# Query and key projection with features on partitions, block-matrix mean squares, and weight low parts on GpSimd

## The chip, the cores and the metric

The kernel runs on one core of a Trainium2 chip. The metric is the device time of one launch in microseconds (us). The engines of the core are TensorE (PE in the profile; PEld is its weight load), VectorE (DVE), ScalarE (ACT), GpSimd (POOL) and SyncE (SP), which here only issues DMAs. Each engine takes its instructions in order; a "q" behind an engine's name means its queue. SBUF is the on-chip memory with 128 partitions, PSUM the memory into which TensorE accumulates.

## What is computed

One layer of a hybrid decoder on 1024 tokens with 1024 features, all in fp32. Cut to what matters here:

```python
h = rms_norm(x, attn_norm_w)
proj = h @ w_in                              # 7168 columns
q, k, v, u, g = jnp.split(proj, splits, axis=-1)
q = rms_norm(q.reshape(B, S, N_HEADS, 2, HEAD_DIM), q_norm_w)   # HEAD_DIM = 64
k = rms_norm(k.reshape(B, S, N_HEADS, 2, HEAD_DIM), k_norm_w)
# two softmaxes per head, over q1.k1 and q2.k2, each with a causal T5 bias; 8 heads
p = probs(qb1, k1f) - lamf * probs(qb2, k2f)
a = rms_norm(p @ v, subln_w) * (1.0 - lam_init)
# branch B: u_a * sigmoid(u_b), depthwise causal convolution of width 31, layer norm, silu, projection
# x + (g_a * y_a + g_b * y_b) @ w_out, then x + SwiGLU(rms_norm(x))
```

So each head has 128 columns of q and 128 of k, and each 64 of them are normalized by their own root mean square.

## The kernel before

**Products in three parts.** Each fp32 factor is split in a high part (fp32r, a cast on ScalarE, `split_hi`, L120) and a low part (source minus high part; `split_lo` on VectorE, L125, or GpSimd, L131, by the switch `low_by_pool` in `low`). A product is hi*hi + hi*lo + lo*hi, three matmuls for each slice of 128 along the contraction (`mm3`, L168 to L170). Two forms exist: `gemm_T` keeps 128 weight columns stationary and streams 512 tokens (the result has features on partitions); `gemm_N` keeps 128 tokens stationary and streams 256 weight columns (the result has tokens on partitions).

**Weights** come through the stream `ws`: a raw tile of 128x1024 by DMA on SP, the cast, the low part, in tiles `whi` and `wlo` of three buffers each; `ws.ahead` says how many are prepared in advance. `ld_cols` loads 128 columns whole, `ld_wide` 256 columns in two halves of the contraction.

**Stages.** First the norm of x, its transposes (`hT_hi`, `hT_lo`), v of the first columns; then v, and the u columns (`u_pair`, by a scheme of seven products per 2x2 blocks, L980), while the depthwise convolution runs on VectorE as background work `bg`: 31 taps (`conv_taps`, L594) for each of eight channel tiles. Taps of the first four tiles accumulate in PSUM (`CONV_PSUM = 4`), those of the others in SBUF. Through this stage `low_by_pool` is true. Then q and k of head 0 and the last v columns (`last`), then the attention.

**Attention** is a loop of 64 steps (8 heads x 8 tiles of 128 queries). A step does the scores of one tile (`scores`: two matmuls for each 512 keys, the bias and minimum on VectorE L1291, the exponential on ScalarE L1296, the difference of the two softmaxes on VectorE L1304 and L1306), turns the weights of the tile before (`turn`: transposes L1328, split L120 and L125), now and then sums v by them (`weigh`) and normalizes a head (`subln`, L1362), and takes a group of "fill" work from `later`: q and k of the next head (`q_item`) and the gate columns (`g_item`), 6 or 8 groups for each head. `turn` clears parts of `ph` and `pl` on GpSimd (L1318, L1319). The remaining 127 pieces of background work, taps of the last four tiles, are shared among the steps by a table of slack: `slack_of` estimates TensorE's and VectorE's time of each step. `low_by_pool` is false from here on.

**q and k of a head** (`q_item`): for each half of 512 tokens, four tiles of 128 tokens by `gemm_N` with 128 q and 128 k columns side by side; a copy to `qkraw` (L797), 16 sums of squares on ScalarE for each two tiles (L800), the root on VectorE and ScalarE (`rstd_of`, `rsq`), the scaling on VectorE (L807). `turn_qk` then transposes four 128x128 tiles on TensorE into PSUM (L815), and from there makes the high and low parts (L822, L824, L835), which DMAs on SP copy between the partition halves (8 for q, 2 for k). These are queued in `late` with the step from which their buffers are free.

A planner of the framework simulates the program and sets the order of instructions on each engine; `after(...)` in the code holds an instruction behind a given one. What the planner sets may differ between two programs in places that the diff does not name.

Of the kernel before, what the change touches and what calls it, by code (L numbers as in the profile page):

```python
# [16 lines left out]
P = 128  # L17
S = 1024
D = 1024
H = 8  # L20
# [37 lines left out]
def kernel(  # L58
# [170 lines left out]
    def load_vectors():  # L229
        pool.memset(rows[:], 0.0)  # L230
        pool.dma_start(cwrow[:], conv_w[0])
# [16 lines left out]
    neglam = cst.tile([P, 1], F32, name="neglam")  # L248
    lprod = ap.tile([P, 2, HD], F32, name="lprod", bufs=1)
# [34 lines left out]

    def wtiles():
        return [wp.tile([P, 1024], F32R, tag=t_, name=nm(t_)) for t_ in ("whi", "wlo")]
# [31 lines left out]
    def ld_wide(w, cols):  # L318


        def half(g):
            def go():
# [11 lines left out]
                hi, lo = wsplit(raw)  # L334
# [80 lines left out]

    def loads_of(it):
        c = int(it[1:])
        if it[0] == "V":
            return ld_wide(win, [(V0 + 256 * c, 256)])
# [224 lines left out]
    def rsq(v, n, fast):  # L644

        r = sm.tile([P, 16], F32, tag="r", name=nm("r"))[:, :n]
        t = sm.tile([P, 16], F32, tag="t", name=nm("t"))[:, :n]
# [32 lines left out]
    def rstd_of(ss, n, scale, fast=False):  # L680
        v = sm.tile([P, 16], F32, tag="v", name=nm("v"))[:, :n]
        dve.tensor_scalar(v, ss, scale, EPS, op0=ALU.mult, op1=ALU.add)
        return rsq(v, n, fast)
# [101 lines left out]

    def q_item(h):
        halves = [ws.next(), ws.next()]
        t = {}
        T[h] = t
        for b in (1, 0):  # L790
            raw = qkp.tile([P, 4, 256], F32, tag="qkraw", name=nm("qkraw"), bufs=2)
            ss = sm.tile([P, 16], F32, tag="ss16", name=nm("ss16"))
            for i2 in range(2):
                o = pg()
                for e in range(2):
                    gemm_N(o[:, 256 * e : 256 * (e + 1)], halves, hT_hi, hT_lo, 4 * b + 2 * i2 + e)
                act.copy(raw[:, 2 * i2 : 2 * i2 + 2, :], o[:].rearrange("p (e c) -> p e c", c=256))  # L797
                jk = sm.tile([P, VD], F32, tag="jk", name=nm("jk"), bufs=1)[:, :HD]
                for g in range(8):
                    act.activation(  # L800
                        jk, o[:, g * HD : (g + 1) * HD], AF.Square, accum_out=ss[:, 8 * i2 + g : 8 * i2 + g + 1]
                    )
                if i2 == 0:
                    yield
            r = rstd_of(ss[:], 16, 1.0 / HD, fast=h > 0)
            r4 = raw[:].rearrange("p i (g d) -> p (i g) d", d=HD)
            dve.tensor_tensor(r4, r4, r.unsqueeze(2).to_broadcast([P, 16, HD]), op=ALU.mult)  # L807

            def turn_qk(z, key, b, raw):


                dma = nc.sync.dma_start
                pt = pm("pQ")
                for i in range(4):
                    pe.transpose(pt[:, i * P : (i + 1) * P], raw[:, i, z * P : (z + 1) * P], ident[:])  # L815
                w = pcol(key + "n")

                def part(j):
                    return qkp.tile([P, 512], F32R, tag=f"{key}s{j}", name=f"{key}s{j}_{h}_{b}", bufs=2 if key == "q" else 3)

                s1, s2 = part(1), part(2)
                act.activation(s1[:], pt[:], AF.Identity, scale=w)  # L822
                lo = part(3) if key == "q" else qkp.tile([P, 512], F32R, tag="klo", name=f"klo_{h}_{b}", bufs=1)
                dve.scalar_tensor_tensor(lo[:], pt[:], w, f32(s1[:]), op0=ALU.mult, op1=ALU.subtract)  # L824
                if key == "q":
                    dma(f32(s2[HD:, :]), f32(s1[HD:, :]))
                    lo2 = part(4)
                    for one, two in ((s1, s2), (lo, lo2)):
                        if one is lo:
                            dma(f32(two[HD:, :]), f32(one[HD:, :]))  # L830
                        dma(f32(two[:HD, :]), f32(one[HD:, :]))
                        dma(f32(one[HD:, :]), f32(one[:HD, :]))
                    t["q", b] = (s1, lo), (s2, lo2)
                else:
                    act.activation(s2[HD:, :], pt[HD:, :], AF.Identity, scale=w[HD:, :])  # L835
                    dma(f32(s2[:HD, :]), f32(lo[HD:, :]))
                    dma(f32(s1[HD:, :]), f32(lo[:HD, :]))
                    t["k", b] = s1, s2

            for z, key in ((1, "k"), (0, "q")):
                free = NT * (h - 1) + (0 if key == "k" and b else NT if key == "q" and not b else NT // 2)
                late.append((free if h else 0, lambda a_=(z, key, b, raw): turn_qk(*a_)))
            yield
# [400 lines left out]
    while late:  # L1246
        late.pop(0)[1]()
# [887 lines left out]
```

## Time and profile before

| | us |
|---|---|
| median of 3 runs | 1726.78 |
| lowest, highest | 1726.03, 1735.44 |
| profiled execution, first to last instruction (span) | 1725.7 |
| TensorE busy | 1714.6 |
| VectorE busy | 1275.4 |
| ScalarE busy | 862.5 |
| GpSimd busy | 219.1 |

The span is of one profiled execution; its own time is not listed apart from it, and the median of the runs is 1.1 us above it. Busy time of TensorE counts matmuls from start to modelled end, and these overlap, so that it says little on how dense they stand; the distance from one start to the next does. In a row of a group, the first number behind the bar is the busy time of all instructions of the group in us, the second the mean of one in ns, the third the idle time of the engine ahead of them, with what ended it. In the chain, a row has its start, its length, and the group with its count. In the timeline, a row has its start and length in us, the engine, line, operation, and tiles, out<-in. The windows show the busy time of each engine in a stretch.

### The profile page before, as it was taken

How to read it: one execution, taken by the hardware profiler on the slowest of the kernel's cores; microseconds unless marked ns; L12 is line 12 of the kernel's file. 1: busy time of each engine (PE TensorE's matmuls, PEld its weight loads, DVE VectorE, ACT ScalarE, POOL GpSimd, SP SyncE). 2: the span in 40 equal slices, each digit the busy share in tenths (PEclk: the TensorE clock that was granted, in tenths of full speed). 3: DMA queues.
4: the chain of work that ended last, by engine and by line, in shares of the span. 5: the costliest groups of instructions: out<-in, count | busy, mean ns of one | idle time of the engine just before them, and what ended most of it. 6: DMA issues, size and time to landing. Idle time of an engine off the chain costs nothing.

```text
span 1725.7 us, 25863 instructions
## 1 busy us (share of the span) xinstructions
PE 1714.6 (99%) x9243; PEld 1477.9 (86%) x9243; DVE 1275.4 (74%) x2128; ACT 862.5 (50%) x1958; POOL 219.1 (13%) x207
## 2 busy tenths in 40 slices
PE   9999999999999999999999999999999999999999
PEld 7997889998998998988788888888888888888887
DVE  7675889898988888878687769966676666575544
ACT  5333335767777776756556325633333333333332
POOL 3997851000000000000000000000000000000000
PEclk9999999999999999999999999999999999999999
DMA  6344445336345344343973683245455445598663
GB/s 208 116 126 132 131 151 154 104 109 171 104 127 147 115 125 138 101 136 130 333 238 118 200 296 119 74 135 164 147 170 170 154 141 164 175 355 285 217 215 130
DMA packets 261604, 281.64 MB, mean 163 GB/s; under 512 B 16546, under 2 KB 181986, under 8 KB 261475
## 3 DMA queue, kind: packets, MB, share of 16 engines
q1 hardware_dynamic: 254160, 267.71, 48.3%
q0 software_dynamic: 5680, 9.39, 2.6%
q10 hardware_dynamic: 1634, 2.89, 0.5%
q8 instruction: 73, 1.20, 0.3%
q14 instruction: 57, 0.46, 0.1%
HBM read 181.84 MB, written 85.50 MB: 155 GB/s over the span
## 4 chain that ended last, share of the span: by engine, by line
PE 92%; DMA 3%; DVE 2%; ACT 1%; issue 1%; POOL 0%; SPq 0%; DVEq 0%; POOLq 0%; ACTq 0%
PE acc L980 29%; PE acc L488 12%; PE pg L168 12%; PE pg L169 12%; PE pg L170 12%; PE wo L1850 3%; PE sc L1290 2%; PE sc L1289 2%; PE pT L1328 2%; PE pg L1106 1%; DVE acc L594 1%; PE pW L168 1%; PE pW L169 1%; PE pW L170 1%; PE pQ L815 1%
## 5 line engine op out<-in xcount | busy, mean ns | idle before, releaser
L594 DVE SCALAR_TENSOR_TENSOR acc<-u,cw,acc 128x1023 f32<-128x1023 f32 (+14 forms) x240 | 303.4, 1264 | 23.2 <-ACT acc L588 20.7
L170 PE MATMUL pg<-whi,hT_lo 128*128 128x256 f32 x704 | 200.2, 285 | 0.0
L168 PE MATMUL pg<-whi,hT_hi 128*128 128x256 f32 x704 | 199.7, 285 | 0.4 <-DVE v L125 0.4
L169 PE MATMUL pg<-wlo,hT_hi 128*128 128x256 f32 x704 | 199.5, 284 | 0.0
L125 DVE TENSOR_TENSOR wlo<-draw,whi 128x1024 fp32r<-128x1024 f32 x75 | 91.7, 1223 | 83.4 <-ACT whi L120 78.9
L120 ACT CAST whi<-draw 128x1024 fp32r<-128x1024 f32 x75 | 79.1, 1055 | 129.5 <-PE acc L488 114.3
L169 PEld LDWEIGHTS pg<-wlo,hT_hi 128*128 128x128 f32 x704 | 134.4, 191 | 1.8
L170 PEld LDWEIGHTS pg<-whi,hT_lo 128*128 128x128 f32 x704 | 134.3, 191 | 1.8
L168 PEld LDWEIGHTS pg<-whi,hT_hi 128*128 128x128 f32 x704 | 134.0, 191 | 2.1 <-DVE v L125 0.6
L120 ACT CAST whi<-wraw 128x1024 fp32r<-128x1024 f32 x90 | 94.7, 1052 | 70.6 <-PE pg L169 32.6
L488 PE MATMUL acc<-wlo,whi 128*128 128x512 f32 x308 | 119.8, 389 | 0.0
L488 PE MATMUL acc<-whi,wlo 128*128 128x512 f32 x308 | 119.8, 389 | 0.0
L1296 ACT ACTIVATE E<-E,mn 128x640 f32<-128x640 f32 (+7 forms) x128 | 99.8, 781 | 30.8 <-DVE mn L1291 29.2
L168 PE MATMUL pg<-hT_hi,whi 128*128 128x512 f32 x288 | 114.4, 397 | 0.1
L169 PE MATMUL pg<-hT_lo,whi 128*128 128x512 f32 x288 | 113.7, 395 | 0.0
L170 PE MATMUL pg<-hT_hi,wlo 128*128 128x512 f32 x288 | 113.7, 395 | 0.0
L120 ACT CAST whi<-s 128x1024 fp32r<-128x1024 f32 x54 | 56.9, 1053 | 104.9 <-PE acc L980 101.8
L125 DVE TENSOR_TENSOR wlo<-wraw,whi 128x1024 fp32r<-128x1024 f32 x75 | 93.3, 1246 | 12.6 <-ACT whi L120 12.3
L1291 DVE CUSTOM_DVE_ANT_0 E<-sc,tb 128x512 f32<-128x512 f32 (+3 forms) x128 | 74.2, 585 | 33.2 <-PE pT L1328 16.1
L980 PE MATMUL acc<-h_hi,whi 128*128 128x512 f32 x240 | 93.4, 389 | 0.0
L980 PE MATMUL acc<-h_lo,whi 128*128 128x512 f32 x240 | 93.4, 389 | 0.0
L980 PE MATMUL acc<-h_hi,wlo 128*128 128x512 f32 x240 | 90.1, 389 | 0.0
(370 smaller groups left out, 4589.7 us busy)
## 6 DMA issues: line engine op xcount, KB each, us to landing
wraw<-in_w_gate_up_dram SPq DMA_DIRECT2D x44, 512.0 KB, 4.7
wraw<-in_w_in_dram SPq DMA_DIRECT2D x38, 512.0 KB, 4.0
qs<-qs SPq DMA_DIRECT2D x96, 128.0 KB, 2.3
wd<-in_w_down_dram SPq DMA_DIRECT2D x44, 256.0 KB, 3.1
tdT<-wd SPq DMA_DIRECT2D x88, 128.0 KB, 4.8
draw<-sdS SPq DMA_DIRECT2D x44, 256.0 KB, 3.7
draw<-tdT SPq DMA_DIRECT2D x44, 256.0 KB, 3.7
wraw<-in_w_in_dram SPq DMA_DIRECT2D x32, 256.0 KB, 3.3
```

The source lines that it names most:

```text
L120: act.copy(dst, src)
L125: last_lo[0] = dve.tensor_tensor(dst, src, f32(hi), op=ALU.subtract).ins
L168: pe.matmul(o, lh, rh, start=start, stop=False)
L169: pe.matmul(o, lh, rl, start=False, stop=False)
L170: last_mm[0] = pe.matmul(o, ll, rh, start=False, stop=stop).ins
L488: m = pe.matmul(o[s_][i][:], l_[:, ts], r_[:, 512:], start=start and j + y_ == 0, stop=j == n - 1 and y_ == 2, skip_group_check=not start,)
L594: dve.scalar_tensor_tensor(a_, us[c][:, : S - n], cw[:, c, t : t + 1], a_, op0=ALU.mult, op1=ALU.add)
L980: last_mm[0] = pe.matmul(o[:], a_[x_][:, k, :], b_[y_][:, k, :], start=start and k + x_ + y_ == 0, stop=k == 3 and x_ == 1, skip_group_che ...
L1289: pe.matmul(o[:, :w], qh[:, qs], k, start=True, stop=False)
L1291: dve.tensor_tensor_reduce(e[:, ks], o[:, :w], tb[:, S - nk + c0 : S - nk + c0 + w], 1.0, mn[:, j : j + 1] if c0 else 3.0e38, ALU.add, ALU ...
L1296: act.activation(e[:, :nk], e[:, :nk], AF.Exp, bias=mn[:, j : j + 1], scale=-1.0, accum_out=l[:, j : j + 1])
L1850: last_mm[0] = pe.matmul(o[s_][i][:], A[u_], B[v_], start=start and j + y_ == 0, stop=j == 3 and y_ == 2, skip_group_check=not start,).ins
```

## The change

- `q_item` computes q and k by `gemm_T`: for k, then q, two halves of 512 tokens each; the weights are two loads of 128 columns (`ld_cols`) in place of two halves of 256. Each result is copied to a tile `raw` of 128 features x 512 tokens. No transposes remain in `turn_qk`; it reads `raw` in SBUF where it read PSUM.
- Mean squares: `qk_step`, once a step, takes one `raw`: the square and its upper bound (`BIGSQ`) on GpSimd, the high part on ScalarE, the low part on GpSimd. A step later (`LAG = 1`) `norm_qk` multiplies both by `halfmean`, a matrix of two 64x64 blocks of -0.5/64, so that PSUM holds -0.5 times the mean square of each feature's half on every partition; ScalarE takes the logarithm and the exponential, GpSimd scales `raw`, and three operations on VectorE do one Newton step.
- Low parts of weights stay on GpSimd through the attention (`low_by_pool` is reset only behind it).
- Buffers: three places of weight tiles by number; two serve as weights in the attention, with one tile ahead, the third as room for the squares and roots. The low and high parts of one v weight lie in the `pl` tile.
- The table of ScalarE's logarithm and exponential is loaded ahead of head 0's q and k. `slack_of` has new constants for VectorE.

```diff
     def loads_of(it):
...
         if it[0] == "Q":
-            return ld_wide(win, [(Q0 + c * P, P), (K0 + c * P, P)])
+            return ld_cols(win, K0 + c * P) + ld_cols(win, Q0 + c * P)
...
     def q_item(h):
...
+        T[h] = {}
+        for key in "kq":
+            w = ws.next()
+            for b in (1, 0):
+                o = gemm_T(w, hT_hi, hT_lo, b)
+                raw = qkp.tile([P, 512], F32, tag="raw", name=f"raw{key}{h}_{b}", bufs=4)
+                act.copy(raw[:], o[:])
+                raws.append((h, key, b, raw))
+                yield
...
+    def qk_step(n):
+        while norms and norms[0][0] <= n - LAG:
+            norm_qk(*norms.pop(0)[1])
+        if raws and len(norms) < 2:
+            h, key, b, raw = raws.pop(0)
+            hi, lo, place = q_room(F32R)
+            sq = apl[0].tile([P, 512], F32, tag="at", name=nm("sq"), bufs=2)[:]
+            pool.tensor_tensor(sq, raw[:], raw[:], op=ALU.mult)
+            pool.tensor_scalar(sq, sq, BIGSQ, None, op0=ALU.min)
+            split_hi(hi, sq)
+            pool.tensor_tensor(lo, sq, f32(hi), op=ALU.subtract)
+            norms.append((n, (h, key, b, raw, hi, lo, place)))
+
+    def norm_qk(h, key, b, raw, hi, lo, place):
+        pt = pm("pN")
+        pe.matmul(pt[:], halfmean[:], hi, start=True, stop=False)
+        last_mm[0] = pe.matmul(pt[:], halfmean[:], lo, start=False, stop=True).ins
+        r, t, _ = q_room(F32, place)
+        act.activation(r, pt[:], AF.Ln, scale=-2.0, bias=eps[:])
+        act.activation(r, r, AF.Exp, scale=-0.5)
+        pool.tensor_tensor(raw[:], raw[:], r, op=ALU.mult)
+        dve.scalar_tensor_tensor(t, pt[:], -0.5 * EPS, r, op0=ALU.add, op1=ALU.mult)
+        dve.tensor_tensor(t, t, r, op=ALU.mult)
+        dve.scalar_tensor_tensor(raw[:], t, 1.5, raw[:], op0=ALU.add, op1=ALU.mult)
...
     def turn_qk(h, key, b, raw):
...
+        act.activation(s1[:], raw[:], AF.Identity, scale=w)
...
+        dve.scalar_tensor_tensor(lo[:], raw[:], w, f32(s1[:]), op0=ALU.mult, op1=ALU.subtract)
...
     def first_stage():
...
-        ws.ahead = 2
+        tc.keep_in_program_order(act.preload_act_table_set("natural_log_exp_and_others"))
+        with after(last_of(mybir.EngineType.Activation)):
+            make_neglam()
+        wplace[0] = cycle((0, 1))
+        ws.ahead = 1
...
-    low_by_pool[0] = False
     pcv_ctx.close()
...
     def slot(n, nq):
         with after(last_fill[0]):
+            qk_step(n)
...
     def slack_of(n):
...
-        t_dve = 0.4 + 4.2e-3 * nk + p + 0.3
+        t_dve = 0.7 + 4.2e-3 * nk
+        if n < NT * (H - 1):
+            t_dve += (0.7, 3.5, 2.6, 1.9, 2.5, 1.4, 0.0, 0.0)[n % NT]
...
+        if n == NT * (H - 1) + 1:
+            wplace[0], ws.ahead = cycle((2, 1 - wlast[0], wlast[0])), 2
...
     inatt[0] = False
+    low_by_pool[0] = False
```

More of the change, by code (lines that the diff above doesn't have):

```diff
@@ L333, in go @@
                     o += n
-                hi, lo = wsplit(raw)
+                hi, lo = wsplit(raw, tiles[g])
                 return (
@@ L784 @@
     late = []
+    BIGSQ = 3.3e38
+    raws, norms, LAG = [], [], 1
     def q_item(h):
[L787 to L845, printed above, removed]
@@ L1245 @@
         due -= int(due)
+    while norms or raws:
+        qstep[0] += 1
+        qk_step(qstep[0])
     while late:
         late.pop(0)[1]()
-    low_by_pool[0] = False
     pcv_ctx.close()
```

68 lines of the change are left out of this document (55 added, 13 removed).

## Prediction

> **What bounds the kernel now.** I read the page's totals and the chain first, then the chain in order of time, then the busy times of the attention stretch.
>
> ```profile
> span 1725.7 us, 25863 instructions
> PE 1714.6 (99%) x9243; PEld 1477.9 (86%) x9243; DVE 1275.4 (74%) x2128; ACT 862.5 (50%) x1958; POOL 219.1 (13%) x207
> ...
> PE 92%; DMA 3%; DVE 2%; ACT 1%; issue 1%; POOL 0%; SPq 0%; DVEq 0%; POOLq 0%; ACTq 0%
> ```
>
> ```profile
> 147.85 94.99 PE acc L980 x418
> ...
> 405.06 0.44 PE pQ L815 x4
> ```
>
> ```profile
> core 0: us, PE busy (x) PEld busy (x) DVE busy (x) ACT busy (x) POOL busy (x), PEclk, DMA share, GB/s
> 240.00:306.00 66.00, 65.64 (x516) 63.99 (x515) 56.87 (x63) 32.98 (x104) 15.09 (x10) 1.00 0.65 181
> 306.00:812.00 506.00, 503.77 (x3366) 460.90 (x3366) 437.17 (x972) 358.84 (x1186) 17.88 (x69) 1.00 0.43 122
> ```
>
> TensorE holds 92% of the chain, at a granted clock of 1.00. A matmul row lasts longer than its turn, because matmuls overlap; the turn is what counts. In the chain 418 matmuls of 512 columns take 94.99 us, so one turn is 0.227 us. The 506 us from 306 to 812 are the attention, in which q and k of heads 1 to 7 are made, one head during the one before it: 63 us for each of 8 heads. There VectorE is busy 437.2 us, 86%, so it has only 68.8 us of idle time, and GpSimd has almost nothing to do (17.9 us). Time goes down if TensorE has fewer turns, as long as VectorE's 437 us and what it waits for stay under TensorE's time. That is the question of this change.
>
> **TensorE's sum.**
>
> ```profile
> 65.74 0.28 PE L169 MATMUL pg<-wlo,hT_hi 128*128 128x256 f32 x1
> ...
> 72.46 0.28 PE L168 MATMUL pg<-whi,hT_hi 128*128 128x256 f32 x1
> ```
>
> Between these two rows of the timeline lie 56 turns of 256 columns: 6.72 us, 0.120 us each. So two narrow turns (0.240) cost little more than a wide one (0.227), although their rows have long durations.
> - q and k: out go 8 heads x 8 token tiles x 8 slices x 3 = 1536 turns at 0.120, 184.3 us. In come 8 x 2 x 2 x 24 = 768 turns at 0.227, 174.5 us. Gain 9.8.
> - Transposes: out go 128 at 0.11 (0.44 for 4 in the chain), 14.1 us.
> - Mean squares: in come 64 products of 512 columns with the block matrix at 0.227, 14.5 us.
>
> Net 9.4 us less, 8.2 of them in the attention and 1.2 for head 0 ahead of it. TensorE alone would take 498 us in the attention.
>
> **ScalarE** loses the sums of squares:
>
> ```profile
> L800 ACT ACTIVATE jk<-pg 128x64 f32<-128x64 f32 x220 | 49.8, 226 | 4.8
> L800 ACT ACTIVATION_READ_ACCUMULATOR jk<-pg 128x1 f32 x220 | 43.9, 199 | 0.0
> L1296 ACT ACTIVATE E<-E,mn 128x512 f32<-128x512 f32 x16 | 11.6, 723 | 3.8 <-DVE mn L1291 3.8
> ```
>
> 93.7 us go. For each of the 28 blocks (7 heads, q and k, two halves) come a split, a logarithm and an exponential of 512 columns, at most 28 x 3 x 0.72 = 61 us. It was busy 359 of 506 us; it falls to some 326 and bounds nothing. The table load that moves ahead costs nothing there, for the same reason.
>
> **VectorE's own work** in the attention:
>
> ```profile
> L594 DVE SCALAR_TENSOR_TENSOR acc<-u,cw,acc 128x1023 f32<-128x1023 f32 (+14 forms) x120 | 151.2, 1260 | 2.9 <-ACT acc L588 2.8
> ...
> L1306 DVE SCALAR_TENSOR_TENSOR E<-E,rl,E 128x640 f32<-128x640 f32 (+7 forms) x63 | 51.6, 819 | 0.6
> ...
> L125 DVE TENSOR_TENSOR wlo<-wraw,whi 128x1024 fp32r<-128x1024 f32 x29 | 35.4, 1219 | 2.8 <-ACT whi L120 2.7
> ...
> L807 DVE TENSOR_TENSOR qkraw<-qkraw,r 128x1024 f32<-128x1024 f32 x14 | 17.0, 1218 | 0.0
> ...
> L1304 DVE SCALAR_TENSOR_TENSOR rl<-rl,neglam,l 128x1 f32<-128x1 f32 x64 | 13.7, 214 | 0.5
> L824 DVE SCALAR_TENSOR_TENSOR qs<-pQ,pvec,qs 128x512 fp32r<-128x512 f32 x14 | 10.4, 746 | 4.6 <-ACT qs L822 4.6
> ...
> L1362 DVE TENSOR_TENSOR an<-an,r 128x1024 f32<-128x1024 f32 x7 | 8.5, 1216 | 0.0
> L656 DVE TENSOR_SCALAR t<-t 128x16 f32<-128x16 f32 (+1 forms) x21 | 3.6, 173 | 0.2
> ```
>
> ```profile
> L963 DVE TENSOR_TENSOR s<-wraw,wraw 128x512 f32<-128x512 f32 x20 | 13.7, 684 | 0.0
> ```
>
> Out: the weights' low parts (35.4), the scaling of the raw tiles (17.0), and for 14 row norms five small operations of about 0.17, as L656 (11.9): 64.3 us. In: for each of 28 blocks two SCALAR_TENSOR_TENSOR of 512 columns (0.746, as L824) and one TENSOR_TENSOR (0.684, as L963): 61 us. VectorE's own work goes from 437 to 434 us. By itself that changes nothing.
>
> **GpSimd's new work, and what it does to VectorE.** GpSimd's rows from ahead of the attention, and its memsets in it:
>
> ```profile
> L131 POOL TENSOR_TENSOR wlo<-wraw,whi 128x1024 fp32r<-128x1024 f32 x15 | 36.2, 2414 | 49.6 <-ACT whi L120 49.6
> ...
> L131 POOL TENSOR_TENSOR sl<-wraw,sh 128x512 fp32r<-128x512 f32 x7 | 9.2, 1307 | 1.6 <-ACT sh L120 1.6
> ```
>
> ```profile
> L1319 POOL MEMSET pl<- 128x128 f32 x30 | 6.2, 206 | 440.2 <-PE pW L169 348.7 <-PE pW L170 38.1 <-DVE rl L1304 20.5
> ```
>
> 29 low parts at 2.41 are 70 us. Each of 28 blocks has three two-input operations of 512 columns (square, low part of the square, raw times r) at 1.31 and one minimum. The trace has no such minimum: between 0.21 (a memset of 128 columns) and 1.31 I take 1.0, nearer to the row of the same width. 28 x 4.93 = 138. Together 208 us (186 to 217) in 506: GpSimd itself has room. But see both engines where they met before:
>
> ```profile
> 46.60 9.47 POOL L896 TENSOR_TENSOR F<-hT_hi,hT_lo 128x1024 f32<-128x1024 f32 x4
> 56.04 9.09 POOL L905 TENSOR_TENSOR F<-F,F 128x1024 f32<-128x1024 f32 x3
> ...
> 271.12 4.77 POOL L131 TENSOR_TENSOR wlo<-wraw,whi 128x1024 fp32r<-128x1024 f32 x2 [17.17 <-ACT whi L120]
> ```
>
> ```profile
> 48.42 0.69 DVE L125 TENSOR_TENSOR vl<-pg,vh 128x512 fp32r<-128x512 f32 x1 [2.02 <-ACT vh L120]
> 49.02 4.78 DVE L272 TENSOR_TENSOR lprod<-lamt 128x64 f32<-128x64 f32 x2
> ...
> 56.94 2.57 DVE L125 TENSOR_TENSOR wlo<-wraw,whi 128x1024 fp32r<-128x1024 f32 x1
> ...
> 273.47 1.26 DVE L594 SCALAR_TENSOR_TENSOR acc<-u,cw,acc 128x1009 f32<-128x1009 f32 x1
> 274.65 2.31 DVE L807 TENSOR_TENSOR qkraw<-qkraw,r 128x1024 f32<-128x1024 f32 x1
> ```
>
> Two products of only 64 columns took 4.78 us beside L896: each stood for one whole GpSimd operation. L807 took 2.31 beside L131 where its group in the attention has 1.22, and the low part at 56.94 took 2.57 against 1.22. Each of these has both inputs in SBUF. The split at 48.42 and the tap at 273.47 (its acc is one of the four PSUM accumulators) read one input from PSUM and lost nothing. So while GpSimd reads SBUF, a VectorE operation with two SBUF inputs stands still until GpSimd's operation is over. The attention's taps (L594, accumulators in SBUF there), L1306, L1304, L1362 and the new operations with two SBUF inputs (TENSOR_TENSOR, the last SCALAR_TENSOR_TENSOR, and L824, which now reads SBUF) come to 151.2 + 51.6 + 13.7 + 8.5 + 28 x (0.684 + 0.746 + 0.746) = 286 us, 57% of the stretch. No row shows a large SCALAR_TENSOR_TENSOR with two SBUF inputs beside a reading GpSimd: its wait lies between nothing and that of the TENSOR_TENSOR rows. I take theirs, as the nearest form.
>
> The Trainium skill, "SBUF — State Buffer", section "Who interferes with whom", says that any VectorE instruction with two SBUF inputs contends with a GpSimd instruction that reads SBUF, and that the second one waits for the whole of the first. By that rule the taps wait too, and the sum is the one below; without it, it is that of the first rival. The rows above agree for TENSOR_TENSOR; none here shows it for the taps.
>
> How much of GpSimd's 208 us VectorE loses lies between none (each falls under an operation that reads PSUM, or idle time) and all. L807 lost 1.09 of an operation of 2.4, 0.46; the low part at 56.94 lost 1.35, 0.56. I take 0.5: 104 us.
>
> **The sum.** VectorE needs 434 + 104 = 538 us in the attention, TensorE 498. VectorE becomes the bound: its idle 69 us are gone and the stretch grows from 506 to 538, by 32 us. The gain of 8.2 is hidden under this. Ahead of it (240 to 306), where head 0 is made and the taps still accumulate in PSUM, VectorE gets 4 x 2.18 = 8.7 us and loses two L807 (2.31 and 1.22) and ten small operations (1.7): 3.5 more, with 9 idle; TensorE gains 1.2. I take 0 (-1.2 to +3.5). The new slack table moves taps to the last head, which the sum over all eight already allows. Behind 812 nothing changes in amount. The profiled execution's span is 1725.7, and the median, 1726.8, lies 1.1 above it, which I take as what surrounds the span: 1725.7 + 32 + 1.1 = **1759 us**. If VectorE cannot be filled beyond 94%, as in its fullest stretch here,
>
> ```profile
> 350.00:400.00 50.00, 50.00 (x363) 47.15 (x362) 46.88 (x96) 36.62 (x132) 1.71 (x7) 1.00 0.42 117
> ```
>
> it is 572 for 538, +66, 1793. The forecast's own range is 1736 to 1790.
>
> **Costed at nothing.** The 8 and 2 DMAs of each turned q and k block stay on SP, in the same number. The two halves of a wide weight load become two loads of the same bytes. The products with the block matrix are the added wait: behind them in TensorE's queue stand all later matmuls. They come a step (63 / 8 = 7.9 us) after the squares, whose chain on GpSimd and ScalarE is 1.31 + 1.0 + 0.72 + 1.31 = 4.3 us; if it is later than a step, TensorE waits for the rest. One weight ahead in place of two: a tile serves two steps, 15.8 us.
>
> ```profile
> L120 ACT CAST whi<-wraw 128x1024 fp32r<-128x1024 f32 x29 | 30.5, 1052 | 16.4 <-PE pg L169 13.5 <-PE pg L170 2.8
> ```
>
> ```profile
> wraw<-in_w_in_dram SPq DMA_DIRECT2D x38, 512.0 KB, 4.0
> ```
>
> Cast 1.05, load 4.0 and low part 2.41 are 7.5 us, which TensorE's matmuls of those two steps cover; with no cover each tile costs up to 7.5.
>
> **Rivals.**
> 1. *Only TENSOR_TENSOR waits; SCALAR_TENSOR_TENSOR does not.* Then the port touches L1362 and the new TENSOR_TENSOR, 28 us, plus small ones: 35 operations with at most 2.4 each, 84 us at worst and some 30 likely, where 498 - 434 = 64 are free. TensorE stays the bound: 1726.8 - 9.4 = 1717.4. For: only TENSOR_TENSOR is shown waiting. Against: the other form also reads two tensors from SBUF. It decides for "not slower". Chance 0.25, of which 0.17 are over 0.5% faster.
> 2. *The waits fall mostly into idle time.* At a lost share under (498 - 434) / 208 = 0.31 TensorE remains the bound (1717.4); up to 0.39 the time stays within 0.5% (8.6 us). For: taps often alternate with score operations that read PSUM. Against: 0.46 and 0.56 above. Chance 0.17: 0.06 faster, 0.11 the same.
> 3. *Low parts stick in GpSimd's queue.* The memsets of ph and pl wait for TensorE's weighted sums (440 us idle before 30 of them, 14.7 each); the engine takes its instructions in order, so a low part, and a square, behind such a memset waits too, and TensorE waits for the weight. With 8 us to spare per tile a stuck one costs some 7; a quarter of 29 costs 50: about 1767. Against: the planner can place a low part ahead of the memset. Chance 0.08, slower.
>
> The forecast has 0.50. Faster by over 0.5%: 0.17 + 0.06 = 0.23. Within 0.5%, about what a measurement of this kernel can tell from no change: 0.08 + 0.11 = 0.19. Slower: 0.50 + 0.08 = 0.58. The range 1714 to 1788 takes in rival 1 with its small spread and nearly all of the forecast's own range.
>
> **What would show it.** In the changed profile: pg groups of q and k at 512 columns, no pQ transposes, 1536 fewer narrow turns (right or wrong at once). Taps with a mean well over 1.26 us, and L1306's over 0.82, where GpSimd's share is high: the forecast's mechanism. Taps at 1.26: rival 1. VectorE over 95% busy from 306 on and TensorE's idle waits named DVE: the bound has moved. Waits of TensorE for GpSimd's low parts: rival 3. The forecast is wrong if the taps keep their duration, or if their waits stay under 64 us in all.

## The result, and the profile after

The changed kernel takes 1812.5 us (median of 4 runs, 1808.9 to 1813.1) beside 1726.4 us for the kernel before: a ratio of 1.048, 95% interval 1.0449 to 1.0511. It is 86 us slower. The forecast of 1759 us had the direction; the time lies above its range (1714 to 1788).

The page of the kernel after: totals, and the shares of the chain that ended last.

```profile
span 1807.1 us, 23873 instructions
...
PE 1750.3 (97%) x8411; PEld 1449.3 (80%) x8411; DVE 1357.0 (75%) x2096; ACT 844.0 (47%) x1511; POOL 489.6 (27%) x369
...
PE 54%; DVE 11%; DMA 2%; issue 2%; ACT 2%; POOL 0%; SPq 0%; DVEq 0%; ACTq 0%; POOLq 0%
```

In after the chain could be followed back only to 489.7 us, so its shares add up to 71% where those of before add up to 99%: 54% beside 92% is no fall of that size. Of the part that is covered TensorE has 54 of 71 and VectorE 11 of 71, where VectorE had 2 of 99. The windows of the kernel after, columns as in the prediction (PE, PEld, DVE, ACT, POOL, clock, DMA):

```profile
240.00:306.00 66.00, 66.00 (x383) 58.16 (x382) 60.66 (x61) 27.07 (x39) 38.77 (x28) 1.00 0.53 151
306.00:884.00 578.00, 531.05 (x2693) 441.81 (x2691) 518.04 (x946) 347.08 (x809) 264.12 (x210) 0.95 0.40 112
```

The attention takes 578 us in place of 506. VectorE's busy time rose from 437 to 518 us, and 60 us of idle time remain of 68.8. TensorE's granted clock is 0.95 where it was 1.00. VectorE's groups in that stretch:

```profile
L614 DVE SCALAR_TENSOR_TENSOR acc<-u,cw,acc 128x994 f32<-128x994 f32 (+14 forms) x121 | 182.8, 1511 | 7.8 <-ACT acc L608 7.5
L1337 DVE CUSTOM_DVE_ANT_0 E<-sc,tb 128x512 f32<-128x512 f32 (+3 forms) x128 | 74.3, 582 | 22.0 <-DMA tb<-t_d 8.9 <-PE sc L1336 8.0 <-PE pT L1374 3.9
L1352 DVE SCALAR_TENSOR_TENSOR E<-E,rl,E 128x640 f32<-128x640 f32 (+3 forms) x64 | 62.7, 979 | 0.9
...
L1350 DVE SCALAR_TENSOR_TENSOR rl<-rl,neglam,l 128x1 f32<-128x1 f32 x64 | 27.5, 430 | 0.8
L852 DVE TENSOR_TENSOR qroom<-qroom 128x512 f32<-128x512 f32 x28 | 27.5, 981 | 0.2
L851 DVE SCALAR_TENSOR_TENSOR qroom<-pN,qroom 128x512 f32<-128x512 f32 x28 | 19.1, 683 | 0.7 <-ACT qroom L849 0.7
...
L869 DVE SCALAR_TENSOR_TENSOR klo<-rawk,pvec,ks 128x512 fp32r<-128x512 f32 x14 | 14.9, 1061 | 2.2 <-ACT ks L867 2.2
L853 DVE SCALAR_TENSOR_TENSOR rawq<-qroom,rawq 128x512 f32<-128x512 f32 x14 | 13.2, 943 | 2.3 <-POOL rawq L850 1.2
L869 DVE SCALAR_TENSOR_TENSOR qs<-rawq,pvec,qs 128x512 fp32r<-128x512 f32 x14 | 13.1, 935 | 3.2 <-ACT qs L867 3.2
L853 DVE SCALAR_TENSOR_TENSOR rawk<-qroom,rawk 128x512 f32<-128x512 f32 x14 | 11.7, 833 | 0.5
```

The taps went from 1260 to 1511 ns, L1352 (L1306 before) from 819 to 979, L1350 from 214 to 430. L851, of the same width as L853 but with one input in PSUM, stays at 683. L1337, which reads the scores from PSUM, stays too (582 ns; L1291 before, 585). What lengthens reads two tensors from SBUF, and only where GpSimd reads at the same time: in the trace half of the taps lie beside such an operation of GpSimd and take 1765 ns on the mean, the other half 1262; L851 has 683 and 680. A small exception is L676, a TENSOR_SCALAR with one tensor from SBUF: the one of its seven that lies beside such a read takes 1.05 us, the others 0.17. Two places of the timeline, VectorE's rows first:

```profile
598.58 1.49 DVE L614 SCALAR_TENSOR_TENSOR acc<-u,cw,acc 128x995 f32<-128x995 f32 x1
...
600.40 3.37 DVE L614 SCALAR_TENSOR_TENSOR acc<-u,cw,acc 128x994 f32<-128x994 f32 x1
603.69 0.99 DVE L1350 SCALAR_TENSOR_TENSOR rl<-rl,neglam,l 128x1 f32<-128x1 f32 x1
```

```profile
600.33 2.39 POOL L131 TENSOR_TENSOR wlo<-wraw,whi 128x1024 fp32r<-128x1024 f32 x1 [1.03 <-DMA qs<-qs]
602.68 1.99 POOL L836 TENSOR_TENSOR sq<-rawk 128x512 f32<-128x512 f32 x1
```

A tap that starts just behind a low part on GpSimd ends 3.37 us later, and L1350, with one element in each partition, ends when the next GpSimd operation does (604.67). GpSimd's groups:

```profile
L131 POOL TENSOR_TENSOR wlo<-wraw,whi 128x1024 fp32r<-128x1024 f32 x30 | 76.3, 2542 | 120.8 <-ACT whi L120 105.4 <-PE sc L1336 12.8 <-issue 1.6
L837 POOL TENSOR_SCALAR sq<-sq 128x512 f32<-128x512 f32 x27 | 51.6, 1914 | 1.2
L839 POOL TENSOR_TENSOR qroom<-sq,qroom 128x512 fp32r<-128x512 f32 x28 | 43.1, 1541 | 54.3 <-ACT qroom L120 54.3
L850 POOL TENSOR_TENSOR rawq<-rawq,qroom 128x512 f32<-128x512 f32 x14 | 20.8, 1486 | 39.3 <-ACT qroom L849 39.3
L850 POOL TENSOR_TENSOR rawk<-rawk,qroom 128x512 f32<-128x512 f32 x14 | 20.1, 1439 | 37.8 <-ACT qroom L849 37.8
L836 POOL TENSOR_TENSOR sq<-rawk 128x512 f32<-128x512 f32 x13 | 19.2, 1480 | 12.4 <-ACT rawk L817 7.0 <-DMA a_d<-at 5.2
L836 POOL TENSOR_TENSOR sq<-rawq 128x512 f32<-128x512 f32 x14 | 18.9, 1348 | 1.1 <-ACT rawq L817 1.1
```

These operations, all of which read SBUF, come to 250 us. VectorE's rows above, against their durations before (and 746 ns for L853 and L869, 684 for L852), lost 30.4 + 10.2 + 13.8 + 8.3 + 4.0 + 7.1 = 74 us, nearly 80 with the small ones. The largest waits of TensorE's weight loads in the stretch:

```profile
PEld sc L1335 <- DVE mn L1337: 32.0, 27, 3.6
PEld pT L1374 <- DVE E L1352: 6.9, 1, 6.9
```

TensorE waits for VectorE, in the place where the next scores need a PSUM bank that VectorE has yet to read. In the trace of before the same wait has 0.4 us:

```profile
PEld sc L1289 <- DVE mn L1291: 0.4, 2, 0.3
```

### The profile page after: what moved, and what is told of

Read it like the earlier page. It is cut to its first block, busy times and chain, and to the rows that moved or that the text cites. A ratio compares the mean times of both kernels' runs of the same rounds, so it can differ in the third digit from the quotient of the medians.

```text
span 1807.1 us, 23873 instructions
## 1 busy us (share of the span) xinstructions
PE 1750.3 (97%) x8411; PEld 1449.3 (80%) x8411; DVE 1357.0 (75%) x2096; ACT 844.0 (47%) x1511; POOL 489.6 (27%) x369
## 3 DMA queue, kind: packets, MB, share of 16 engines
q1 hardware_dynamic: 253904, 267.71, 46.7%
## 4 chain that ended last, share of the span: by engine, by line
PE 54%; DVE 11%; DMA 2%; issue 2%; ACT 2%; POOL 0%; SPq 0%; DVEq 0%; ACTq 0%; POOLq 0%
PE acc L1020 21%; PE acc L508 12%; PE pg L168 5%; PE pg L169 5%; PE pg L170 5%; DVE acc L614 3%; PE wo L1897 3%; DVE E L1337 2%; DVE E L1352 1%; DVE pl L125 1%; DMA tb<-t_d 1%; ACT E L1342 1%; DVE qroom L852 1%; DVE rl L1350 1%; PE sc L1335 0%
## 5 line engine op out<-in xcount | busy, mean ns | idle before, releaser
L168 PE MATMUL pg<-hT_hi,whi 128*128 128x512 f32 x544 | 220.5, 405 | 0.0
L169 PE MATMUL pg<-hT_lo,whi 128*128 128x512 f32 x544 | 219.7, 404 | 0.0
L170 PE MATMUL pg<-hT_hi,wlo 128*128 128x512 f32 x544 | 218.7, 402 | 0.0
L125 DVE TENSOR_TENSOR wlo<-draw,whi 128x1024 fp32r<-128x1024 f32 x75 | 91.8, 1224 | 84.8 <-ACT whi L120 78.9
L131 POOL TENSOR_TENSOR wlo<-wraw,whi 128x1024 fp32r<-128x1024 f32 x44 | 110.1, 2503 | 135.2 <-ACT whi L120 119.8
L170 PEld LDWEIGHTS pg<-hT_hi,wlo 128*128 128x128 f32 x544 | 105.5, 194 | 21.6
L168 PEld LDWEIGHTS pg<-hT_hi,whi 128*128 128x128 f32 x544 | 105.8, 195 | 20.9 <-DVE v L125 0.2
L169 PEld LDWEIGHTS pg<-hT_lo,whi 128*128 128x128 f32 x544 | 105.5, 194 | 20.2
L1335 PE MATMUL sc<-ks,qs 128*128 128x512 f32 (+2 forms) x192 | 71.4, 374 | 25.5 <-DVE mn L1337 23.2
L1337 DVE CUSTOM_DVE_ANT_0 E<-sc,tb 128x512 f32<-128x512 f32 (+3 forms) x128 | 74.3, 582 | 22.0 <-DMA tb<-t_d 8.9
L508 PE MATMUL acc<-whi 128*128 128x512 f32 x308 | 84.1, 389 | 0.0
L125 DVE TENSOR_TENSOR wlo<-s,whi 128x1024 fp32r<-128x1024 f32 x40 | 49.0, 1225 | 32.0 <-ACT whi L120 32.0
```

Source lines behind the costliest of these rows:

```text
L125: last_lo[0] = dve.tensor_tensor(dst, src, f32(hi), op=ALU.subtract).ins
L131: pool.tensor_tensor(dst, src, f32(hi), op=ALU.subtract)
L168: pe.matmul(o, lh, rh, start=start, stop=False)
L169: pe.matmul(o, lh, rl, start=False, stop=False)
L170: last_mm[0] = pe.matmul(o, ll, rh, start=False, stop=stop).ins
L508: m = pe.matmul(o[s_][i][:], l_[:, ts], r_[:, 512:], start=start and j + y_ == 0, stop=j == n - 1 and y_ == 2, skip_group_check=not start,)
```

## The experiments

Twelve kernels ran. Two tables sum them up. In the second, "attention" is a window from the first score product to 13 us behind the last one (for before that is the window of the prediction), "DVE" VectorE's busy time in it, and "stall" the sum of TensorE's distances from start to start beyond a usual turn (227 ns for 512 columns, 170 for 384, 120 for 256, 110 for 128) between those two products, counted from the trace: its waits and its slow turns.

| kernel | us | ratio to before (95%) |
|---|---|---|
| after | 1812.5 | 1.048 (1.0449 to 1.0511) |
| e1_write_only | 1752.7 | one execution |
| e2_align | 1808.3 | 1.048 (1.0464 to 1.0496) |
| e3_before_shift | 1738.5 | 1.0085 (1.0063 to 1.0107) |
| e4_all_vector | 1801.7 | one execution |
| e5_low_vector | 1804.0 | one execution |
| e6_before_low | 1739.3 | 1.0074 (1.0059 to 1.0089) |
| e7_align512 | 1797.3 | 1.0409 (1.0392 to 1.0427) |
| e8_no_gpsimd | 1748.2 | 1.013 (1.0115 to 1.0145) |
| e9_one_product | 1735.2 | 1.0052 (1.0036 to 1.0069) |
| e10_three_places | 1730.6 | 1.0024 (1.0013 to 1.0035) |
| e11_late_product | 1740.0 | 1.0075 (1.0059 to 1.0092) |
| e12_taps_as_e10 | 1741.8 | 1.0081 (1.0064 to 1.0098) |

| kernel | attention | DVE | DVE idle | mean tap, ns | stall |
|---|---|---|---|---|---|
| before | 506 | 437.2 | 68.8 | 1260 | 18.8 |
| e6 | 520 | 453.8 | 66.2 | 1342 | 28.8 |
| e1 | 516 | 440.4 | 75.6 | 1263 | 35.9 |
| e8 | 527 | 450.7 | 76.3 | 1261 | 45.2 |
| e4 | 557 | 519.9 | 37.1 | 1264 | 76.8 |
| e5 | 565 | 507.9 | 57.1 | 1338 | 84.8 |
| e7 | 572 | 518.3 | 53.7 | 1496 | 91.4 |
| after | 572 | 517.0 | 55.0 | 1513 | 92.1 |

**GpSimd's reads.** The same instructions on GpSimd, but they only write:

```diff
-        if low_by_pool[0]:
+        if low_by_pool[0] == "write":
+            pool.memset(f32(dst), 0.0)
+        elif low_by_pool[0]:
...
-            pool.tensor_tensor(sq, raw[:], raw[:], op=ALU.mult)
-            pool.tensor_scalar(sq, sq, BIGSQ, None, op0=ALU.min)
+            pool.memset(sq, 1.0)
...
-            pool.tensor_tensor(lo, sq, f32(hi), op=ALU.subtract)
+            pool.memset(f32(lo), 0.0)
...
-        pool.tensor_tensor(raw[:], raw[:], r, op=ALU.mult)
+        pool.memset(raw[:], 0.0)
...
+    low_by_pool[0] = "write"
```

> The changed kernel, where from the attention's start every GpSimd operation on weights, squares and roots is a memset of the same output tile: it writes SBUF but reads nothing. Left out: the low parts, the squares and the scaling by r (the outputs are not the reference's). Theory 'port' (a VectorE operation with two SBUF inputs stands still while GpSimd reads SBUF): the taps go back from 1.51 to 1.26 us each, VectorE needs 434 us for the 573 us stretch and TensorE becomes the bound again: 1725 to 1745 us. Rival 'chain and buffers' (one weight ahead in place of two, the step-long chain squares, products, root, one bias tile): the taps may shorten, but the time stays above 1785 us.

Measured: 1752.7 us, 59.8 below after: 8 above the range of the theory (1725 to 1745), which had nothing in it for the addresses (below), and 32 under the rival's 1785. The taps among VectorE's groups in the attention of e1, and GpSimd's largest group there:

```profile
L616 DVE SCALAR_TENSOR_TENSOR acc<-u,cw,acc 128x1023 f32<-128x1023 f32 (+14 forms) x118 | 149.1, 1264 | 10.3 <-ACT acc L610 10.2
```

```profile
L131 POOL MEMSET wlo<- 128x1024 f32 x30 | 28.8, 959 | 146.7 <-PE pg L172 132.1 <-ACT sgg L661 6.6 <-DVE mn L1339 5.2
```

Beside 82 us of writes by GpSimd the taps have their old duration. So it is the reads that hold VectorE, and with them go 60 of the 86 us. The Trainium skill, "SBUF — State Buffer", section "Who interferes with whom", says this of a GpSimd instruction that reads SBUF and excepts one that only writes it: the taps agree, with 1511 ns beside reads in after and 1264 beside writes here. GpSimd's time is shorter too in e1 (82 us against 264), so what GpSimd's own lateness adds isn't separated here.

**Who does the work.** In e4 the whole chain and the weights' low parts go to VectorE; in e5 the low parts alone, the last line of this diff:

```diff
-            pool.tensor_tensor(sq, raw[:], raw[:], op=ALU.mult)
-            pool.tensor_scalar(sq, sq, BIGSQ, None, op0=ALU.min)
+            dve.tensor_tensor(sq, raw[:], raw[:], op=ALU.mult)
+            dve.tensor_scalar(sq, sq, BIGSQ, None, op0=ALU.min)
...
-            pool.tensor_tensor(lo, sq, f32(hi), op=ALU.subtract)
+            dve.tensor_tensor(lo, sq, f32(hi), op=ALU.subtract)
...
-        pool.tensor_tensor(raw[:], raw[:], r, op=ALU.mult)
+        dve.tensor_tensor(raw[:], raw[:], r, op=ALU.mult)
...
+    low_by_pool[0] = False
```

> The changed kernel with all its attention work for GpSimd (low parts of the weights, squares, their bound and low part, scaling by r) on VectorE. VectorE's own work in the attention rises by 29 x 1.22 + 28 x (3 x 0.68 + 0.6) = 109 us to some 543, and the waits for GpSimd (some 80 us) are gone. Theory 'port': the sum of own work and waits rises from 514 to 543, and the time stays about the same or rises a little: 1805 to 1850 us, with taps at 1.26. Rival 'GpSimd's queue is late' (weights and roots arrive late because GpSimd is slow or waits in order): the time falls below 1790.

> The changed kernel with the weights' low parts back on VectorE in the attention; squares and roots stay on GpSimd. In the changed kernel VectorE lost some 80 us to 250 us of GpSimd work, 0.32 of it; 76 us of this are low parts, so 24 us of waits go and 29 x 1.22 = 35 us of own work come. Theory 'port' with this share: VectorE has 11 us more to do, 1812 to 1825 us. Rival 'waits fall on long operations' (a low part of 2.4 us costs VectorE more than half of itself): the time falls to 1790 to 1805.

Measured: 1801.7 and 1804.0 us, 11 and 8.5 below after. e4 is a little below the 1805 of its theory and well above the rival's 1790, so by that sign GpSimd's lateness isn't the main cost. e5 missed its theory (1812 to 1825) and lies where its rival has it (1790 to 1805): a low part costs VectorE more than half of its own length, as e6 shows next. Nothing waits for the port in e4 (taps 1264 ns), and VectorE is busy 519.9 us, as long as in after (517.0). What VectorE loses to GpSimd's reads is about what the same work costs on VectorE itself: GpSimd took nothing off it.

In e6 the kernel before keeps everything but leaves the weights' low parts on GpSimd through the attention:

```diff
-    low_by_pool[0] = False
     pcv_ctx.close()
...
     inatt[0] = False
+    low_by_pool[0] = False
```

> The kernel before with the weights' low parts on GpSimd through the attention, nothing else of the change. VectorE loses 35 us of own work and gets 70 us x 0.3 to 0.6 = 21 to 42 us of waits, so its need stays near 437 of 506 us and TensorE remains the bound. Theory 'port': taps of 1.26 us rise to a mean of 1.33 to 1.45, and the time stays at 1726 within 6 us. Rival 'GpSimd's queue delays the weights': 1740 or more.

Measured: 1739.3 us, 12.6 above before. The theory's time (1726 within 6) is missed, though its taps (1.33 to 1.45 us) came, and the time is almost the rival's (1740 or more); but the rival's cause doesn't show, for none of TensorE's waits in the attention of e6 names GpSimd. From the groups of e6 in the attention, GpSimd's and then VectorE's:

```profile
L131 POOL TENSOR_TENSOR wlo<-wraw,whi 128x1024 fp32r<-128x1024 f32 x28 | 72.9, 2607 | 189.7 <-ACT whi L120 183.7 <-PE sc L1289 2.8 <-DMA ks<-klo 2.1
```

```profile
L594 DVE SCALAR_TENSOR_TENSOR acc<-u,cw,acc 128x1023 f32<-128x1023 f32 (+14 forms) x118 | 158.5, 1344 | 8.5 <-ACT acc L588 8.3
...
L657 DVE TENSOR_TENSOR r<-r,t 128x16 f32<-128x16 f32 (+1 forms) x21 | 11.1, 530 | 0.3
...
L682 DVE TENSOR_SCALAR v<-ssa 128x8 f32<-128x8 f32 x7 | 6.8, 968 | 2.1 <-ACT jk L1356 2.1
```

VectorE is rid of 35 us of subtractions, yet its busy time rises by 17 us. Taps, L1305, the row norms and their small operations wait (L657 has 530 ns where it had 168, L682 968 where it had 164). 72.9 us of GpSimd cost VectorE 35 + 17 = 52 us by its busy time, 45 us if the lengthening is summed row by row: a share of 0.6 to 0.7, while the work itself took 35 us on VectorE. This one part of the change, by itself, makes the kernel slower.

**Addresses.** Behind the attention nothing was to change, but the longest stretch of matmuls there has another pace. From the chain in order of time (start, length, group), before and after:

```profile
1132.43 371.73 PE acc L980 x1640
```

```profile
1205.25 380.11 PE acc L1020 x1644
```

226.7 ns a turn became 231.2. The change adds a tile `eps` of 4 bytes, which takes 32, and so the wide tiles on the left side of SBUF, features and weights, start 32 bytes further (modulo 512), while those of the right side stay. e3 puts 32 bytes into the kernel before; e2 fills 32 bytes up to a multiple of 64 in after (96 more); e7 takes the place for `eps` from `pvec` and pads until the tiles lie as before, modulo 512:

```diff
+    cst.tile([P, 8], F32, name="pad_cst")          # e3, in before
...
+    cst.tile([P, 24], F32, name="pad_cst")         # e2, in after
...
-    sm.tile([P, 32], F32, name="pad_sm", bufs=1)   # e7, in after
+    sm.tile([P, 64], F32, name="pad_sm", bufs=1)
-    eps = cst.tile([P, 1], F32, name="eps")
+    eps = pvec[:, NROW - 1 : NROW]
```

> The changed kernel with 96 idle bytes behind the new 4-byte tile eps (which takes 32), so that all tiles on the left side of SBUF start at multiples of 64 bytes again, as they did before; nothing else. Theory 'address': the 512-column matmuls behind the attention (1644 in 380.1 us of the chain, 231 ns each, where they were 227) go back to 227 ns, the stretch behind the attention loses its 9 us and the one ahead of it 4 to 5: 1797 us (1792 to 1802). Rival 'clock or power' (matmuls slower for another reason, as the granted clock fell in the attention): 1812 +- 3, still 231 ns.

> The kernel before with 32 idle bytes among its constants: the same tiles start 32 bytes off a multiple of 64, nothing else. Theory 'address': matmuls of 512 columns take 228 to 235 ns where they took 227, the time rises by 10 to 25 us to some 1742. Rival: 1726 +- 3.

> The changed kernel with eps in a free column of the constants' tile and 128 more idle bytes among the small tiles, so that all tiles on the left side of SBUF stand a multiple of 512 bytes from where they stood before, and so each pair of matmul operands has the distance modulo 512 that it had before. In the run with 96 idle bytes (multiples of 64, but the weights 128 bytes off a multiple of 512) the slow pairs were those whose two operands differ modulo 256. Theory 'distance of the two operands': all matmuls behind the attention go back to 227 ns; with some 5 us ahead of the attention and 8 within, 1790 to 1803. Rival 'multiples of 64' is already out; rival 'the change's instructions': 231 ns and 1808 to 1812.

Measured: e3 is 12.3 us above before, with nothing else changed; e2 stands 4 us below after, about the spread of its runs, at the same ratio; e7 takes 15.2 us off after. The same row of the chain in e3, in e2, and in e7:

```profile
1135.20 378.93 PE acc L981 x1640
```

```profile
1205.86 378.01 PE acc L1021 x1644
```

```profile
1200.94 372.64 PE acc L1020 x1644
```

231.1, 229.9 and 226.7 ns a turn. Most of these products take one tile of the right side (T1 to T4) and one of the left. In before and e7 the two start 256 bytes apart (modulo 512); in e3, 224; in after, 224, and 352 for T4, whose other tile lies behind the small tiles that the change narrowed; in e2, 128, but still 256 for T4. The products of two tiles of the left side keep the distance 0 in all five. Not the alignment of each tile but their distance decides: e2's tiles are aligned to 64 bytes and still slow, and its products with T4, which kept the distance of before, take 227.6 ns on the mean, those with T1 to T3 232.8 (by the distances of starts in the trace). Ahead of the attention e3 shows the same the other way round: there T1 to T3 are at distance 0 and take 227.2 ns, T4 is at 288 and takes 232.7. 15 of the 86 us are this, most of it behind the attention: from the start of the last score product to that of the last matmul, after has 932.8 us, before 922.4, e7 922.2.

**What else the change brings.** e8 is e7 without any read by GpSimd in the attention: the low parts on VectorE, the squares on ScalarE, no bound, no Newton step.

```diff
-            pool.tensor_tensor(sq, raw[:], raw[:], op=ALU.mult)
-            pool.tensor_scalar(sq, sq, BIGSQ, None, op0=ALU.min)
+            act.activation(sq, raw[:], AF.Square)
             split_hi(hi, sq)
-            pool.tensor_tensor(lo, sq, f32(hi), op=ALU.subtract)
+            dve.tensor_tensor(lo, sq, f32(hi), op=ALU.subtract)
...
-        pool.tensor_tensor(raw[:], raw[:], r, op=ALU.mult)
-        dve.scalar_tensor_tensor(t, pt[:], -0.5 * EPS, r, op0=ALU.add, op1=ALU.mult)
-        dve.tensor_tensor(t, t, r, op=ALU.mult)
-        dve.scalar_tensor_tensor(raw[:], t, 1.5, raw[:], op0=ALU.add, op1=ALU.mult)
+        dve.tensor_tensor(raw[:], raw[:], r, op=ALU.mult)
```

> A version meant to keep what TensorE gains and to leave GpSimd out of the attention: q and k with features on partitions and the block matrix as in the changed kernel, the addresses of e7, the weights' low parts on VectorE, squares on ScalarE (Square), low parts of squares and the scaling by r on VectorE, no Newton step and no upper bound of the squares (both left out), slack table to match. VectorE's own work: 437 - 17 - 12 + 28 x (0.68 + 0.68) = 446 us, without waits; ScalarE some 336; TensorE 9.4 us less. Theory 'port and fill': at 446 of some 490 us VectorE is as full as it was at its fullest, the gain of TensorE is partly kept: 1715 to 1730. Rival 'one weight ahead and the step-long chain cost by themselves' (what e1 had left over its 1726, less the addresses): 1735 to 1745.

Measured: 1748.2 us, above the ranges of theory and rival alike: 49 below e7 but still 22 above before, although TensorE has 4.8 us less work in the attention (468.6 against 473.4: the time between the first and the last score product less the stall; as e6, with the work of before, has 478.1, this count is good to some 5 us). VectorE is busy 450.7 us and idle 76.3: it isn't full, and TensorE stalls 45 us. Two kernels take this apart: e9 forms only one product per block, and e10 gives the weights their three places and two loads ahead again.

```diff
-            act.activation(sq, raw[:], AF.Square)          # e9
-            split_hi(hi, sq)
-            dve.tensor_tensor(lo, sq, f32(hi), op=ALU.subtract)
+            act.activation(hi, raw[:], AF.Square)
...
-        wplace[0] = cycle((0, 1))                           # e10
-        ws.ahead = 1
+        ws.ahead = 2
```

> The kernel of e8_no_gpsimd, and of each block of q or k only the rounded square goes into one product with the block matrix: ScalarE writes the square straight into the float32r tile, and the low part of the square (28 VectorE subtractions of about 0.68 us, 19 us), the split and the second product (28 x 0.23 = 6.4 us of TensorE) are left out, so the mean squares are less exact. Theory A (what is left of e8's 21 us comes from the weights having two places and one load ahead in the attention): only TensorE's share goes, 1741 us (1737 to 1745). Theory B (it comes from the chain raw - square - split - product - rsqrt - turn that VectorE and ScalarE carry inside one step): the shorter chain gives back 12 us or more, 1728 to 1736 us.

> The kernel of e9_one_product, with the weights' three places and two loads ahead through the attention as in the kernel before; the squares and the reciprocal roots lie in the tiles of the attention's output (tag at) in place of the third weight place. Theory A (two places and one load ahead): 8 us or more below e9, near 1728 us, and TensorE's waits for pW, pB and pT in the attention fall with it. Theory B (the chain inside the step): within 3 us of e9. If both together are all that is left, e10 stands near 1718 us: before's 1726.5 less about 11 us of TensorE work, plus what the 28 extra products and waits still cost.

Measured: 1735.2 and 1730.6 us. e9 gives back 13 us: 5.3 of TensorE's own work in the attention (468.6 to 463.3) and 8 of stalls (45.2 to 37.2). That is theory B's sign. But e9 also takes 13.4 us of work off VectorE (450.7 to 437.2), and at the rate of the second table that alone could be most of the gain, so that the shorter chain and the lighter VectorE aren't told apart. e10 gives back 4.6 more, a little over half of what theory A asked for and more than theory B allows. Together they stand 4.2 us above before (interval 2.2 to 6.0) with 10 us less work on TensorE. What is left in e10, among TensorE's weight loads and VectorE's waits in the attention:

```profile
PEld sc L1321 <- DVE mn L1323: 13.7, 15, 2.8
```

```profile
DVE rawq L839 <- ACT rr L838: 13.9, 8, 3.6
```

TensorE still stands for score banks that VectorE frees late, and VectorE stands at its head for ScalarE's root. e11 was to mend the second, e12 to tell its parts apart:

```diff
-        dve.tensor_tensor(raw[:], raw[:], r, op=ALU.mult)   # e11: a step later
+        mults.append((raw, r))
...
-            t_dve += (1.4, 2.0, 1.9, 1.2, 1.4, 1.4, 0.0, 0.0)[n % NT]
+            t_dve += (0.7, 0.0, 1.4, 0.7, 2.1, 0.7, 0.0, 0.0)[n % NT]   # e11; e12 has e10's
```

> The kernel of e10_three_places, with the reciprocal roots in a place of their own (not in the attention output's, where ScalarE waited 17 us for stores to DRAM: at <- a_d<-at 11.8, rr <- a_d<-at 5.3), the VectorE product raw x root one step later than the root (in e10 VectorE stood 13.9 us at its head for ScalarE's root), and the table of VectorE's slack set to that. As in e9 the low part of the squares is left out. Theory (what is left in e10, TensorE waiting 17 us for score banks that VectorE frees late against 6 in before, comes from VectorE standing behind ScalarE's root): sc waits fall to 10 us or less and the time to 1719 to 1725 us, below before. Rival (the waits come from the other chain, the one of the scores and their exponentials, and from where the taps land): the same as e10 within 2 us, 1729 to 1733.

> The kernel of e11_late_product with e10's table of VectorE's slack, and nothing else: the taps land in the steps in which they landed in e10, while the late product and the root's own place stay. As in e9 the low part of the squares is left out. Theory (e11's 9 us over e10 come from where the taps land): 1719 to 1731 us, at or below e10's 1730.6, and at the lower end if the late product takes VectorE's wait for the root away as it was meant to. Rival (they come from the late product and the three raw tiles): 1737 to 1742, as e11.

Measured: 1740.0 and 1741.8 us, both some 10 us above e10. e11 came out as neither its theory (1719 to 1725) nor its rival (1729 to 1733) had it: VectorE's wait for the root did fall, from 13.9 to 5.3 us, and TensorE's for score banks from 13.7 to 11.6, and the time rose all the same. e12 came out as its rival had it (1737 to 1742), so the table isn't the reason. In e12 VectorE waits as long for the root as in e10:

```profile
DVE rawq L812 <- ACT rr L844: 14.3, 7, 3.9
```

e11 and e12 also have three raw tiles in place of four and a place of its own for the root; which of these costs the 10 us wasn't tried. No kernel here beats the one before.

## Why the prediction was right or wrong

- **Direction and mechanism: right.** The forecast was that GpSimd's reads hold VectorE's operations with two SBUF inputs, SCALAR_TENSOR_TENSOR among them, and that TensorE then waits for VectorE. The taps (1260 to 1511 ns), e1 and TensorE's wait for L1337 show it. Rival 1 (taps unchanged) fell. One of the signs named ahead didn't come: VectorE is 90% busy from 306 us on (518.0 of 578), not over 95%.
- **TensorE's sum: right.** 8.2 us less in the attention were forecast; the traces have 473.4 to 466.4, 7.0 less, by a count that is good to some 5 us.
- **VectorE's own work: right.** 434 us were forecast; 518.0 less the 80 of waits is 438.
- **ScalarE: low by 21 us.** 326 were forecast, 347 measured; of 578 us that is no bound, as forecast.
- **GpSimd's time: low by 42 us.** 208 were forecast, 250 measured. The minimum, estimated at 1.0 us, takes 1.91, which is 25 of the 42. The single ones last from 1.49 to 2.51, so that waits for VectorE may be in them.
- **The lost share: high.** 0.5 was taken; 80 of 250 us is 0.32. The two misses nearly cancel: 104 us of waits forecast, 80 measured.
- **The step that failed is the fill:** "VectorE becomes the bound: its idle 69 us are gone". They are not gone. By the measured load and this step the attention would have taken 518 us, 12 more than before; it took 578, 72 more, because 60 us of idle remain. The warning in the sum (a fill of 94%) was the better reading, and it was left outside the forecast; but with the measured load it gives 551 us, still 27 short. VectorE's idle time before is only in part room to be filled: 46.7 of the 68.8 us belong to the hand-overs of each step (transposes, exponential, scores), in which VectorE waits for TensorE and ScalarE. Its three largest waits in the attention of before:

```profile
DVE E L1291 <- PE pT L1328: 16.1, 14, 3.8
DVE rl L1303 <- ACT E L1296: 15.4, 15, 4.0
DVE E L1291 <- PE sc L1290: 15.2, 14, 4.6
```

The second table shows what more load does: VectorE's busy time grows by 80 us from before to after and the attention by 66; from before to e6 by 17 and 14; from e1 to after by 77 and 56; from before to e4, where nothing waits for GpSimd's reads, by 83 and 51. Some 0.6 to 0.8 of every microsecond put on VectorE come out at the end, though it is never full. Load isn't everything: e4 fills 32 of the 69 us and after only 14 at nearly the same busy time, and e8 grows by 21 with 13 us more on VectorE. Why after fills less than e4 stays open. For the same reason **rival 2** fell: the 80 us of waits are what it allowed for a time within 0.5% (0.39 of 208), and the time rose by 86.
- **"Behind 812 nothing changes in amount": right of the work, wrong of the time.** The address of `eps` was costed at nothing; e7 shows 15 us. Without them the time (1797.3) would still lie above the range.
- **One weight ahead, and the added chain, costed at nothing:** at least the first isn't, for the second weight ahead gave back 4.6 us (e10). A shorter chain gave back 13 (e9), but with less work for VectorE and TensorE in it, so its own cost isn't shown.
- **Rival 3** (low parts stuck behind memsets) doesn't show: TensorE's large waits name VectorE.

So of the 86 us, 60 go with GpSimd's reads (e1, where its operations are shorter too), 15 are the addresses (e7), and some 11 remain, to which the weights' two places contribute and perhaps the new chain. These parts weren't all tried together, so that they need not add exactly.

## What to carry to other kernels

Work moved from VectorE to GpSimd that reads SBUF while VectorE works with two SBUF inputs was not free here: cost it on VectorE nearly as if it had stayed there. Idle time of an engine that hands over to others in every step isn't all slack: before counting on it, look at what ends each idle piece. And after any edit that adds a tile, look whether an untouched stage has kept its time per matmul.

## What the hardware showed that was not expected

**The distance of two operands.** A turn of 512 columns takes 226.7 ns where the stationary and the moving tile start 0 or 256 bytes apart modulo 512 (before and e7), and some 233 ns at 128 (e2), 224, 352 (after) and 288 (e3); other distances weren't looked at, and why isn't known.

**The clock falls where TensorE waits.** Windows of the kernel after:

```profile
300.00:350.00 50.00, 41.29 (x181) 33.20 (x180) 42.00 (x57) 21.71 (x36) 26.96 (x18) 0.90 0.46 123
...
400.00:450.00 50.00, 50.00 (x267) 42.54 (x266) 44.78 (x90) 33.87 (x73) 24.94 (x18) 1.00 0.45 133
...
600.00:650.00 50.00, 42.82 (x205) 34.93 (x204) 45.13 (x91) 31.79 (x76) 26.00 (x22) 0.90 0.47 120
```

In the window where TensorE is always busy the clock is 1.00, in the two where it is busy 41 to 43 of 50 us it is 0.90. Inside the groups of q, k and gate products, where nothing is waited for, 52 turns of 512 columns in after last 400 to 480 ns, about twice 227; in before there is none. The Trainium skill, "TensorE: Matmul & The Clock Gate", Part 1, says that the array runs at half its clock after an idle window of some 3.4 us. This trace has the half, but a shorter wait is enough: at 455.4 us TensorE has been idle for 2.05 us, and from 456.0 to 459.4 us the granted clock is 0.50. So a wait can cost twice, once as a wait and again as slow products. At a mean of 0.95 over 578 us that is 29 us at most, an estimate. The 52 turns alone take 10.3 us more than at 227 ns; how much of the 86 us the clock holds in all was not measured.
